# Low halves of weight blocks computed on GpSimd outside the recurrences; memory attention's softmax over two query blocks at a time

## The chip, the cores and the metric

The kernel runs on one NeuronCore of a Trainium2 chip. The metric is device time in microseconds (us) of one execution. Engines are named as in the profile: PE (matmul) with its weight loads PEld, DVE (vector), ACT (scalar), POOL (GpSimd) and SP, which here issues every DMA. SBUF is the on-chip memory of tiles, PSUM the banks into which PE accumulates.

## The reference, cut to what matters

Two layers. In each, one input projection feeds four branches, which are gated, projected, merged and normalised:

```python
for l in range(DEPTH):                       # DEPTH = 2, S = 512 tokens, D = 1024
    h = x @ w_in[l]                          # columns split among the branches
    y_rwkv = rwkv7(...)                      # delta-rule recurrence, 8 heads of 64
    y_mla  = causal_attention(...)           # low-rank latents, 8 heads
    h_c    = val * sigmoid(glu_gate)         # conformer branch
    y_conv = silu(layer_norm(causal_conv31(h_c))) * silu(gate)
    s      = q @ k_mem.T * 128 ** -0.5       # memory attention: 4 heads, 256 memory tokens
    y_mem  = softmax(s) @ v_mem * silu(gate)
    merged = sum(sigmoid(gate_n) * (y_n @ w_o[l, n]) for n in range(4))
    x      = layer_norm(ALPHA * x + merged @ w_out[l])
```

Everything is float32 in the reference.

## The kernel before, in words

**Split products.** PE multiplies in float16, so each float32 operand is carried as two float16 tiles, a high half h and a low half lo, and a product is three matmuls (`mm3`: h times lo, h times h, lo times h). Activations are split once; weights arrive from HBM as float32 blocks and are split on the fly. The blocks are named w0 to w237 in the order in which they are fetched, nearly all of 128x1024 elements or, for the latent projections, of 128x672. The first (w0) and the last three (flag `last`) are split in two pieces, the others whole: 236 low halves up to w234, and 6 for the last three. PE works about 24 matmuls of 512 columns on one full block.

**A weight block's way.** `weights` allocates a raw tile (three buffers), issues the DMA on SP's queue and starts a small task. When the block has landed and one of four h/lo buffer pairs is free, `split` writes h = float16(32 raw) on ACT, then lo = 32 raw - h on DVE in one scalar_tensor_tensor instruction. PE then uses the block, and the raw buffer goes to the block that is three further on.

**What sets the order.** All engines run their instructions in program order. That order comes from a planner in the kernel itself (`Plan`, `Engine`): every instruction is booked with an estimated cost, tasks are generators that run when the planner's clocks say that their inputs are there, and PE's stream of projections is filled in between. In `Engine.__call__` stands the table of costs by engine and operation.

**Fillers.** The convolution is 30 taps for each of four channel groups, DVE instructions `cacc <- hpad, prm, cacc` of 128x512. They are booked as "slack": one at a time when the planner thinks that DVE is free. Four `cacc` finished, `conv_norm` transposes and normalises them, and then the gates and merge products of the convolution's branch can be put on PE.

**The recurrences.** In each layer `begin_rwkv` opens the recurrence's pool and eight units of `rwkv_unit` follow, each with an inverse of 16x16 blocks by forward substitution on POOL (`ZT`, `tmpW`: 28 small instructions a unit). In the profile POOL's work of the two recurrences lies from 270 to some 510 us and from 1020 to some 1280 us. Apart from that POOL does only the reciprocal roots of the norms (`rstd_of`: `rsl` of the latents, `crs` of the convolution, `gr` of the recurrence, `lrs` of the layer's end).

**Memory attention.** `xhead` takes two query blocks of 128 at a time: PE writes both score blocks into one PSUM tile `xs` (128x2x256), and `weigh` makes the softmax of one block after the other: negative maximum `nm` (DVE), exponent with row sum `sm` (ACT), scaled reciprocal (two small DVE instructions), high half of the probabilities (ACT), low half (DVE). Then two DMA transposes bring them into `xT`, which PE reads for `xo`. `weigh` also serves the latent attention (`ms`, `mP`), where it gets one block.

Of the kernel before, what the change touches and what calls it, by code (L numbers as in the profile page):

```python
# [16 lines left out]
AF = mybir.ActivationFunctionType  # L17
ALU = mybir.AluOpType
# [18 lines left out]
WH = 8  # L37
WSCALE = 32.0
PROB = 16384.0
HEADS = 2  # L40
# [210 lines left out]
class Engine:  # L251
# [5 lines left out]
    def __getattr__(self, name):  # L257
        f = getattr(self.eng, name)

        def call(*a, **k):  # L260
            o = k.get("out", a[0] if a else None)
            i = k.get("in_", k.get("in0", a[1] if len(a) > 1 else o))
            n = 1
# [5 lines left out]
            if self.key == "ACT":  # L269
                c = (150 if psum else 115) + 0.83 * n + (150 if regs > 1 else 90 if regs or "accum_out" in k else 0)  # L270
            elif self.key == "POOL":
                c = 420 + 155 * n if k.get("op") == ALU.pow else 235 + 3.5 * n if n < 100 else 250 + 1.6 * n
            elif name == "scalar_tensor_tensor":
                c = 130 + 1.07 * n
            elif name in ("tensor_scalar", "tensor_copy"):
                c = (100 + 0.95 * n if psum else 68 + 0.53 * n) + (145 if regs else 0)
            elif name == "tensor_tensor_scan":
                c = 140 + 2.0 * n
            elif name == "bn_aggr":
                c = 66 + n  # L280
            else:
                c = 75 + 1.04 * n
# [65 lines left out]
def build(ctx: ExitStack, tc: tile.TileContext, A, out, log, slots, dbg=None):  # L348
# [178 lines left out]

    def split(dst_h, dst_l, src, scale=1.0):

        if scale == 1.0:  # L530
            S.copy(dst_h, src)
        else:
            S.activation(dst_h, src, AF.Copy, scale=scale)
        yield
        if scale == 1.0:
            V.tensor_tensor(out=dst_l, in0=src, in1=dst_h, op=ALU.subtract)
        else:
            V.scalar_tensor_tensor(out=dst_l, in0=src, scalar=scale, in1=dst_h, op0=ALU.mult, op1=ALU.subtract)

# [10 lines left out]

    whole = [1]

    def weights(name, src, parts, last=False):
# [8 lines left out]
        def run():  # L562
            e, n = 0, len(parts)
            step = 1 if whole[0] or last else n
            whole[0] = 0
            for a in range(0, n, step):
# [8 lines left out]
                h, lo = h[:, 0:c], lo[:, 0:c]  # L575
                yield from split(h, lo, raw[:, e:e + c], WSCALE)
                e += c
# [158 lines left out]
    def layer_items(l):  # L736
# [66 lines left out]
        def begin_rwkv(get):  # L803
# [64 lines left out]
        def rwkv_unit(j, hf, r, k, v):  # L868
# [444 lines left out]
        def weigh(h, lo, ps, tag):  # L1313

            nm, sm = st("nm" + tag, 1), st("sm" + tag, 1)
            V.tensor_reduce(out=nm, in_=ps, axis=AX.X, op=ALU.max, negate=True)
            yield
            S.activation(ps, ps, AF.Exp, bias=nm, accum_out=sm)
            yield
            V.tensor_scalar(out=sm, in0=sm, scalar1=1.0 / PROB, scalar2=None, op0=ALU.mult)  # L1320
            V.reciprocal(sm, sm)
            yield
            S.activation(h, ps, AF.Copy, scale=sm)
            yield
            V.scalar_tensor_tensor(out=lo, in0=ps, scalar=sm, in1=h, op0=ALU.mult, op1=ALU.subtract)

        ymem = [None] * 4

        def xhead(h, q):
# [3 lines left out]
            for tp in range(2):  # L1333
# [814 lines left out]
```

## Time and profile before

| | |
|---|---|
| median of 3 runs | 1455.22 us (1454.55 to 1455.3) |
| profiled execution, own time | 1457.4 us |
| its span, first to last instruction | 1455.6 us |
| PE busy | 1396.6 us (96%) |
| DVE busy | 1069.8 us (73%) |
| ACT busy | 650.3 us (45%) |
| POOL busy | 242.2 us (17%) |
| mean granted PE clock | 0.985 |

The own time is that of the whole execution, the span is counted from the first to the last instruction; 1.8 us lie around it. In the views a row of a group gives line, engine, operation, output<-inputs, shape and count, then busy time and mean duration of one. A tile's row gives shortest, median and longest duration. L285 is the planner's recording helper, so vector, scalar and GpSimd instructions are told apart by their tiles; L370 and L375 are matmuls and transposes.

### The profile page before, as it was taken

The numbers are of one execution on the slowest core, as the hardware profiler recorded it, in microseconds if no ns is written. First come the engines' busy times: TensorE is split into PE (matmuls) and PEld (weight loads), VectorE is DVE, ScalarE is ACT, GpSimd is POOL, SyncE is SP. The second block draws the span as 40 slices with busy tenths as digits, with TensorE's granted clock in tenths as the row PEclk, the third lists the DMA queues.
The fourth block names the chain that finished last, engine by engine and source line by source line (L and its number), as shares of the span: only waits on it lengthen the run. The fifth ranks groups of instructions, "written<-read, shape, count | busy, mean of one in ns | idle before, by whom it ended". The sixth has DMA issues, their size and how long they took to land. (4 is left out here: it accounts for less than half of the span.)

```text
span 1455.6 us, 29966 instructions
## 1 busy us (share of the span) xinstructions
PE 1396.6 (96%) x12134; PEld 754.1 (52%) x12134; DVE 1069.8 (73%) x2186; ACT 650.3 (45%) x1227; POOL 242.2 (17%) x557
## 2 busy tenths in 40 slices
PE   9999989999999789999999998999999998998997
PEld 6655544455555554444775544444455555554444
DVE  6688878888787876446654888888888868745756
ACT  5556564444443333344265556634444434432340
POOL 0000000355152600000010000000743433110001
PEclk9999999999999989999999999999999999999999
DMA  6445675231321024233443347662122221324331
GB/s 224 147 117 134 143 139 160 68 115 49 114 70 63 7 101 165 98 116 120 137 156 106 98 116 152 140 175 83 65 94 79 87 81 61 106 90 144 132 116 58
DMA packets 126539, 161.04 MB, mean 111 GB/s; under 512 B 83776, under 2 KB 85312, under 8 KB 126400
## 3 DMA queue, kind: packets, MB, share of 16 engines
q1 hardware_dynamic: 126400, 159.12, 36.6%
q8 instruction: 95, 1.56, 0.4%
q14 instruction: 44, 0.36, 0.1%
HBM read 133.39 MB, written 5.24 MB: 95 GB/s over the span
## 5 line engine op out<-in xcount | busy, mean ns | idle before, releaser
L285 DVE SCALAR_TENSOR_TENSOR cacc<-hpad,prm,cacc 128x512 f32<-128x512 f32 x240 | 179.9, 752 | 2.7
L285 ACT ACTIVATE tm<-ps_m,prm 128x512 f32<-128x512 f32 x64 | 44.0, 687 | 190.9 <-PE ps_m L370 180.2
L285 POOL TENSOR_SCALAR ZT<-W 32x256 f32<-32x256 f32 x16 | 12.2, 761 | 588.6 <-DMA W<-scr 362.5
L285 DVE SCALAR_TENSOR_TENSOR mt<-tm,po 128x512 f32<-128x512 f32 x48 | 32.9, 686 | 102.7 <-PE po L370 72.4
L285 POOL TENSOR_TENSOR ZT<-ZT,tmpW 32x14 f32<-32x14 f32 (+6 forms) x224 | 92.8, 414 | 17.6
L285 POOL TENSOR_TENSOR tmpW<-ZT,W 32x14 f32<-32x14 f32 (+6 forms) x224 | 92.3, 412 | 15.6
L370 PEld LDWEIGHTS <-mg 128*128 128x128 f16 x504 | 49.3, 98 | 34.0
L285 ACT ACTIVATE ms<-ms,nmm 128x128 f32<-128x128 f32 (+3 forms) x64 | 32.1, 501 | 18.4 <-DVE nmm L285 18.2
L285 ACT ACTIVATE mP<-ms,smm 128x128 f16<-128x128 f32 (+3 forms) x64 | 33.0, 527 | 13.5 <-issue 8.5
L370 PE MATMUL ms<-kT,qT 96*128 96x128 f16 (+3 forms) x192 | 36.3, 300 | 2.1 <-DMA kT<-xk 1.7
L285 ACT COPY Y<-gb 64x256 f32<-64x256 f32 x32 | 11.7, 367 | 57.6 <-DVE B L285 57.4
L285 POOL TENSOR_SCALAR gr<-gm 128x4 f32<-128x4 f32 x16 | 6.8, 423 | 179.0 <-DVE gm L285 179.0
L285 DVE TENSOR_TENSOR merged<-merged,mt 128x512 f32<-128x512 f32 x48 | 33.7, 703 | 1.7
L285 DVE SCALAR_TENSOR_TENSOR mP<-ms,smm,mP 128x128 f16<-128x128 f32 (+3 forms) x64 | 34.2, 544 | 0.0
L285 POOL TENSOR_SCALAR lrs<-lmv 128x1 f32<-128x1 f32 x4 | 2.2, 543 | 181.5 <-DVE lmv L285 177.3
L370 PEld LDWEIGHTS <-xh 128*128 128x128 f16 x256 | 25.0, 98 | 13.8 <-issue 2.5
L285 DVE TENSOR_REDUCE nmm<-ms 128x1 f32<-128x128 f32 (+3 forms) x64 | 30.4, 481 | 0.8 <-PE ms L370 0.2
L370 PEld LDWEIGHTS <-qT 96*128 96x128 f16 x192 | 17.1, 98 | 17.1 <-issue 3.5
L285 POOL TENSOR_TENSOR lrs<-lrs,mhalf 128x1 f32<-128x1 f32 x8 | 5.9, 742 | 107.0 <-DVE lrs L285 106.7
L285 DVE SCALAR_TENSOR_TENSOR z<-pz,z 128x256 f32<-128x256 f32 (+1 forms) x15 | 7.7, 512 | 20.9 <-PE pz L370 20.9
L285 ACT ACTIVATE mg<-merged 128x512 f16<-128x512 f32 x16 | 10.1, 630 | 28.1 <-DVE merged L285 28.1
L285 DVE SCALAR_TENSOR_TENSOR merged<-tm,po 128x512 f32<-128x512 f32 x16 | 11.0, 686 | 14.2 <-PE po L370 9.3
(1959 smaller groups left out, 4471.3 us busy)
## 6 DMA issues: line engine op xcount, KB each, us to landing
w<-in_w_ch_dram SPq DMA_DIRECT2D x146, 512.0 KB, 4.0
w<-in_w_o_dram SPq DMA_DIRECT2D x32, 512.0 KB, 3.9
w<-in_w_out_dram SPq DMA_DIRECT2D x16, 512.0 KB, 3.4
w<-in_w_lat_dram SPq DMA_DIRECT2D x16, 336.0 KB, 3.7
w<-in_w_mk_dram SPq DMA_DIRECT2D x8, 512.0 KB, 4.1
w<-in_w_mv_dram SPq DMA_DIRECT2D x8, 512.0 KB, 3.4
w<-in_w_qk_dram SPq DMA_DIRECT2D x8, 320.0 KB, 3.4
x<-in_xT_dram SPq DMA_DIRECT2D x8, 256.0 KB, 5.7
```

The costliest lines, as they stand in the source:

```text
L285: return self.plan.keep(f(*a, **k))
L370: plan.keep(nc.tensor.matmul(o, lhsT, rhs, start=start, stop=stop))
```

## The change

**1. Low halves on POOL.** `split` gets a function W. Where W says yes and the planner's clock of POOL is less than POOLED = 4000 ns ahead, lo is made by two POOL instructions instead of one on DVE: raw is multiplied by 32 in place, then lo = raw - h. `weights` passes `not busy and step > 1`: `busy` holds the layer from `begin_rwkv` to the end of its last unit, and step is 1 for the kernel's first block and its last three.

**2. Memory attention.** `weigh` takes the whole tile `xs` of two query blocks: one maximum for both, two exponents, one scaling and one reciprocal for both, two high halves, two low halves.

**3. Planner's costs.** Four of DVE's estimates are other numbers: scalar_tensor_tensor of 1000 elements and more, reciprocal, bn_aggr, and tensor_reduce from SBUF.

```diff
+POOLED = 4000.0
-                c = 130 + 1.07 * n
+                c = 130 + (1.07 if n < 1000 else 1.01) * n
+            elif name == "reciprocal":
+                c = 165
-                c = 66 + n
+                c = 170 + 4 * n
+            elif name == "tensor_reduce" and not psum:
+                c = 250 + 1.04 * n
...
-    def split(dst_h, dst_l, src, scale=1.0):
+    def split(dst_h, dst_l, src, scale=1.0, W=None):
...
-            V.scalar_tensor_tensor(out=dst_l, in0=src, scalar=scale, in1=dst_h, op0=ALU.mult, op1=ALU.subtract)
+            if W and W() and plan.clk["POOL"] < plan.now() + POOLED:
+                G.tensor_scalar(out=src, in0=src, scalar1=scale, scalar2=None, op0=ALU.mult)
+                G.tensor_tensor(out=dst_l, in0=src, in1=dst_h, op=ALU.subtract)
+            else:
+                V.scalar_tensor_tensor(out=dst_l, in0=src, scalar=scale, in1=dst_h, op0=ALU.mult, op1=ALU.subtract)
...
-                yield from split(h, lo, raw[:, e:e + c], WSCALE)
+                yield from split(h, lo, raw[:, e:e + c], WSCALE, lambda: not busy and step > 1)
...
+            busy.add(l)
...
+                busy.discard(l)
...
-            nm, sm = st("nm" + tag, 1), st("sm" + tag, 1)
+            parts = [(ps, h, lo)] if len(ps.shape) == 2 else [(ps[:, b, :], h[:, 256 * b:256 * b + 256], lo[:, 256 * b:256 * b + 256]) for b in range(2)]
+            nm, sm = st("nm" + tag, len(parts)), st("sm" + tag, len(parts))
             V.tensor_reduce(out=nm, in_=ps, axis=AX.X, op=ALU.max, negate=True)
             yield
-            S.activation(ps, ps, AF.Exp, bias=nm, accum_out=sm)
+            for b, (x, _, _) in enumerate(parts):
+                S.activation(x, x, AF.Exp, bias=nm[:, b:b + 1], accum_out=sm[:, b:b + 1])
...
-                for b in range(2):
-                    yield from weigh(P[:, 256 * b:256 * b + 256], P[:, 256 * b + 512:256 * b + 768], ps[:, b, :], f"x{h}{tp}{b}" + t_)
+                yield from weigh(P[:, 0:512], P[:, 512:], ps, f"x{h}{tp}" + t_)
```

In the changed program's order 125 of the low halves stand on POOL as pairs: w1 to w44, w101 to w166 and w220 to w234, without a gap, which is every block outside the two recurrences but the first and the last three. The other 111 of the 236, and the last 6, stay on DVE.

**How the order moves.** On POOL at the program's start, before (w blocks are raw weights, `rsl` is the latents' reciprocal root, `ZT` the first unit of the recurrence):

```order
L285 MEMSET dpad1_132 128x4
L285 ISA
L285 TENSOR_TENSOR rsl_0_626<-ssl_0_556,cst_81 128x8
L285 TENSOR_SCALAR rsl_0_626<-rsl_0_626 128x8
L285 TENSOR_TENSOR rsl_0_626<-rsl_0_626,mhalf_125 128x8
L285 TENSOR_SCALAR ZT_0_3058<-W_0_3057 32x256
```

The same place in the changed program:

```order
L290 MEMSET dpad1_132 128x4
L290 ISA
L290 TENSOR_SCALAR w1_150<-w1_150 128x672
L290 TENSOR_TENSOR w1l0_196<-w1_150,w1h0_195 128x672
L290 TENSOR_SCALAR w2_169<-w2_169 128x672
L290 TENSOR_TENSOR w2l0_249<-w2_169,w2h0_248 128x672
L290 TENSOR_SCALAR w3_220<-w3_220 128x672
L290 TENSOR_TENSOR w3l0_260<-w3_220,w3h0_259 128x672
```

POOL had nothing to do until the latents' norm; now ten pairs, w1 to w10, stand ahead of `rsl` and 34 behind it, up to the first `ZT`.

On DVE in the first layer, where the first attention pair is projected (`vm` values of the memory, `xq` and `xk` low halves of queries and keys, `cacc` taps), before:

```order
L285 SCALAR_TENSOR_TENSOR vm1_0_445<-pmv110_1094,vm1_0_445 128x256
L285 SCALAR_TENSOR_TENSOR w23l0_1171<-w23_1168,w23h0_1170 128x640
L285 SCALAR_TENSOR_TENSOR xq_0_1197<-pq0_0_1182,xq_0_1197 128x512
L285 SCALAR_TENSOR_TENSOR w24l0_1176<-w24_1173,w24h0_1175 128x1024
L285 SCALAR_TENSOR_TENSOR xk_0_1209<-pk0_0_1193,xk_0_1209 128x512
L285 SCALAR_TENSOR_TENSOR w25l0_1207<-w25_1204,w25h0_1206 128x1024
```

And in the changed program:

```order
L290 SCALAR_TENSOR_TENSOR vm1_0_439<-pmv110_1132,vm1_0_439 128x256
L290 SCALAR_TENSOR_TENSOR cacc0_0_781<-hpad0_127,prm0_236,cacc0_0_781 128x512 x2
L290 SCALAR_TENSOR_TENSOR xq_0_1233<-pq0_0_1215,xq_0_1233 128x512
L290 SCALAR_TENSOR_TENSOR xk_0_1245<-pk0_0_1229,xk_0_1245 128x512
L290 SCALAR_TENSOR_TENSOR cacc0_0_781<-hpad0_127,prm0_236,cacc0_0_781 128x512 x3
L290 SCALAR_TENSOR_TENSOR cacc1_0_1152<-hpad1_128,prm0_236,cacc1_0_1152 128x512 x3
```

The weight splits are gone and taps stand in their place: ahead of the first layer's recurrence (its first instruction on DVE, the copy into `V`) there are 91 taps instead of 52, ahead of the second's 90 of that layer's instead of 67. The first layer's fourth `cacc` is now finished in the third unit of the recurrence and not in the last but one.

On POOL at the end of the first layer (`lrs` is the reciprocal root of the layer norm of one token block), in the changed program:

```order
L290 TENSOR_SCALAR w124_8758<-w124_8758 128x1024
L290 TENSOR_TENSOR w124l0_8761<-w124_8758,w124h0_8760 128x1024
L290 TENSOR_SCALAR lrs0_0_8797<-lmv0_0_8796 128x1
L290 TENSOR_TENSOR lrs0_0_8797<-lrs0_0_8797,mhalf_125 128x1
L290 TENSOR_SCALAR w125_8775<-w125_8775 128x1024
L290 TENSOR_TENSOR w125l0_8780<-w125_8775,w125h0_8779 128x1024
L290 TENSOR_SCALAR lrs1_0_8831<-lmv1_0_8830 128x1
L290 TENSOR_TENSOR lrs1_0_8831<-lrs1_0_8831,mhalf_125 128x1
```

Before, the eight `lrs` instructions stood there by themselves; now the first two norms have a pair of a weight block ahead of them.

More of the change, by code (lines that the diff above doesn't have):

```diff
@@ L549, in build @@
     wlive = {"raw": 0, "hl": 0}
-    whole = [1]
+    whole, busy = [1], set()
     def weights(name, src, parts, last=False):
@@ L1322, in weigh @@
             yield
-            S.activation(h, ps, AF.Copy, scale=sm)
+            for b, (x, y, _) in enumerate(parts):
+                S.activation(y, x, AF.Copy, scale=sm[:, b:b + 1])
             yield
-            V.scalar_tensor_tensor(out=lo, in0=ps, scalar=sm, in1=h, op0=ALU.mult, op1=ALU.subtract)
+            for b, (x, y, z) in enumerate(parts):
+                V.scalar_tensor_tensor(out=z, in0=x, scalar=sm[:, b:b + 1], in1=y, op0=ALU.mult, op1=ALU.subtract)
         ymem = [None] * 4
```

## The prediction

> **What bounds the kernel now.** I read the page first: busy shares of the engines.
>
> ```profile
> span 1455.6 us, 29966 instructions
> PE 1396.6 (96%) x12134; PEld 754.1 (52%) x12134; DVE 1069.8 (73%) x2186; ACT 650.3 (45%) x1227; POOL 242.2 (17%) x557
> ```
>
> PE is idle for 1455.6 - 1396.6 = 59.0 us. The change leaves PE's matmuls as they are, so what it can win lies in these 59 us and in slow clock. The second view is what PE waited for, longest first:
>
> ```profile
> PE xo L370 <- DMA xTl<-xP: 6.8, 5, 2.4
> PE w L370 <- DVE cn L285: 2.5, 1, 2.5
> PE pmv L370 <- DVE w126l L285: 1.9, 1, 1.9
> PE tk L375 <- DVE cn L285: 1.3, 1, 1.3
> PE ct L375 <- DVE cn L285: 1.2, 1, 1.2
> PE ps_val L370 <- DVE w11l L285: 1.1, 1, 1.1
> PE pl L370 <- DVE w0l L285: 0.9, 1, 0.9
> PE pl L370 <- DVE w2l L285: 0.6, 1, 0.6
> PE ps_m L370 <- DVE w162l L285: 0.2, 1, 0.2
> ```
>
> Low halves of weights ended only 1.9 + 1.1 + 0.9 + 0.6 + 0.2 = 4.7 us of PE's waits. The work that moves is therefore not itself what PE waits for; a gain must come through DVE's other work. The third view is busy time by stage: the stretches ahead of the two recurrences (convolution and attentions) and the end of the first recurrence. Columns are stretch, length, then busy time of PE, PEld, DVE, ACT, POOL, and the granted clock.
>
> ```profile
> 55.00:265.00 210.00, 202.09 (x1335) 108.57 (x1334) 174.64 (x368) 119.90 (x255) 0.00 (x0) 0.99 0.56 136
> 480.00:535.00 55.00, 43.01 (x850) 28.93 (x847) 41.93 (x121) 17.61 (x37) 20.66 (x55) 0.84 0.18 58
> 800.00:1010.00 210.00, 198.88 (x1244) 99.88 (x1243) 180.73 (x377) 113.88 (x245) 0.00 (x0) 0.99 0.50 125
> ```
>
> Ahead of the recurrences DVE is busy 83 and 86% and idle 35.4 and 29.3 us; POOL does nothing. At 480 to 535 us PE stands idle for 12.0 us at a clock of 0.84: there the first recurrence's last units run with little else to put on PE.
>
> **DVE and POOL at the same time.** The one place where the trace shows both with much to do is the recurrence. First the durations by tile (shortest/median/longest in ns), then the rows around 400 us (start, duration, engine):
>
> ```profile
> L285 DVE TENSOR_TENSOR merged<-merged,mt x48: 691/692/1152, 399.5 to 1407.1; 128x512 f32<-128x512 f32 x48
> L285 POOL TENSOR_SCALAR ZT<-W x16: 605/712/1124, 270.2 to 1264.7; 32x256 f32<-32x256 f32 x16
> L285 POOL TENSOR_TENSOR tmpW<-ZT,W x224: 203/299/1417, 271.2 to 1281.8; 32x14 f32<-32x14 f32 x16, 32x36 f32<-32x36 f32 x16, 32x50 f32<-32x50 f32 x16, 32x56 f32<-32x56 f32 x16
> ```
>
> ```profile
> 399.48 0.61 POOL L285 TENSOR_SCALAR ZT<-W 32x256 f32<-32x256 f32 x1 [10.13 <-DMA W<-scr]
> 399.48 1.15 DVE L285 TENSOR_TENSOR merged<-merged,mt 128x512 f32<-128x512 f32 x1
> 400.91 1.23 DVE L285 SCALAR_TENSOR_TENSOR w70l<-w,w70h 128x1024 f16<-128x1024 f32 x1
> 401.13 1.11 POOL L285 TENSOR_TENSOR tmpW<-ZT,W 32x26 f32<-32x26 f32 x1
> ```
>
> A DVE instruction that reads two SBUF tiles and a POOL instruction do not run together. `merged` took 1.15 us instead of 0.69 while POOL's 0.61 us ran: it lost 0.46, POOL's length less 0.15. The other way round, `tmpW` on 26 columns took 1.11 us because w70's low half was running. Until now POOL's instructions were short, so DVE lost little. The change puts 250 long ones there, and the fillers that take the place of the weight splits on DVE, the taps `cacc <- hpad, prm, cacc`, read two SBUF tiles each.
>
> The Trainium skill, SBUF — State Buffer, section Who interferes with whom, says the same more strictly: the shared port pair is locked for the whole instruction and the other engine blocks fully. By that the loss would be the whole POOL instruction, 0.15 us more at each meeting, and the sum below about 12 us higher; the row with 0.46 of 0.61 decides for the smaller figure.
>
> **Price of a pair on POOL.** No row shows 128x1024 on POOL. The nearest, without DVE in the way:
>
> ```profile
> 349.71 0.22 POOL L285 TENSOR_TENSOR tmpW<-ZT,W 32x14 f32<-32x14 f32 x1
> 478.65 0.31 POOL L285 TENSOR_TENSOR tmpW<-ZT,W 32x56 f32<-32x56 f32 x1
> L285 POOL TENSOR_SCALAR crs<-cmv 128x1 f32<-128x1 f32 x8 | 1.5, 191 | 25.4 <-DVE cmv L285 25.3
> 398.08 1.06 ACT L285 ACTIVATE w70h<-w 128x1024 f16<-128x1024 f32 x1 [0.54 <-DMA w<-in_w_o_dram]
> ```
>
> The subtraction: (0.31 - 0.22)/42 = 2.1 ns a column, so 0.31 + 968 x 2.1 ns = 2.4 us; from below, 1.23 us, what DVE needs for the same tile. The multiplication: from 191 ns at one column to 605 at 256, 1.62 ns a column, so 1.85 us at most (strided there); from below, ACT's 1.06. I take 2.4, since it is the same operation on the same engine, and 1.4, about the middle, since ZT's source is strided. A pair is then 3.8 us, between 2.3 and 4.3, against 1.2 on DVE.
>
> By the Trainium skill, GPSIMD Engine Reference, section 3. Performance versus the Vector engine, a two-input add of 2048 elements takes 4497 ns; an estimate from that is 2.25 us for the subtraction, and with its near line-rate for one input about 1.05 for the multiplication. With these the sum below would be about +2 instead of +19; no run here shows either.
>
> **The change part by part.** Loss of DVE by a pair: between the convolution's first product and the recurrence the changed order has 321 DVE instructions, 114 of which read two SBUF tiles: a chance of 0.36 each. One lasts 174.64/368 = 0.47 us in the mean. Behind a POOL instruction of length P, DVE loses P - 0.15 if its next instruction is such a one, 0.47 less for each other instruction that comes first. For 2.4 us that is 0.36 x 2.25 + 0.23 x 1.78 + 0.15 x 1.31 + 0.09 x 0.84 + 0.06 x 0.37 = 1.5 us, for 1.4 us 0.7, together 2.2, and with DVE busy 83% of the time 1.8 us a block. What DVE is spared, and what the taps cost:
>
> ```profile
> 60.00:265.00 205.00, 0.00 (x0) 0.00 (x0) 40.89 (x36) 35.15 (x36) 0.99 0.56 135
> 800.00:1010.00 210.00, 0.00 (x0) 0.00 (x0) 38.28 (x33) 32.65 (x33) 0.99 0.50 125
> L285 DVE SCALAR_TENSOR_TENSOR cacc<-hpad,prm,cacc 128x512 f32<-128x512 f32 x240 | 179.9, 752 | 2.7
> L285 DVE TENSOR_REDUCE nmx<-xs 128x1 f32<-128x256 f32 x32 | 13.2, 416 | 0.7 <-PE xs L370 0.7
> L285 DVE RECIPROCAL smx<-smx 128x1 f32<-128x1 f32 x32 | 5.2, 164 | 1.1
> L285 DVE TENSOR_SCALAR smx<-smx 128x1 f32<-128x1 f32 x32 | 4.6, 144 | 0.0
> ```
>
> The first two rows are the weight instructions alone in the two stretches: 40.89/36 = 1.14 and 38.28/33 = 1.16 us of DVE a block.
>
> *First stretch*, blocks w14 to w44, 31 pairs: loss 31 x 1.8 = +56; splits gone -31 x 1.14 = -35; the joint softmax halves the small instructions, (5.2 + 4.6)/2 over two layers, and spares a maximum's fixed part (416 ns - 256 columns at 1.04, 0.15 us, eight times), about -4 a layer; 39 taps come in from the recurrence, 39 x 0.75 = +29. DVE's load grows by 46 us and 35.4 were idle. An engine that is behind doesn't wait any more, so I let three quarters of the idle time take it up, 26: DVE, and PE which needs DVE to empty PSUM, come out +20 us late. Bounds: 46 - 35 = +11 and +46.
>
> *Second stretch*, w140 to w166, 27 pairs: +49 - 31 - 4 + 23 taps x 0.75 = +17 makes +31, against 29.3 idle, three quarters 22: +9, between +2 and +31.
>
> *Start*: w1's and w2's low halves are on PE's path.
>
> ```profile
> 8.05 0.76 ACT L285 ACTIVATE w1h<-w 128x672 f16<-128x672 f32 x1 [0.20 <-DMA w<-in_w_lat_dram]
> 8.85 0.86 DVE L285 SCALAR_TENSOR_TENSOR w1l<-w,w1h 128x672 f16<-128x672 f32 x1
> 9.86 0.31 PE L370 MATMUL pl<-w1l,xh 128*128 128x336 f16 x1
> 13.11 0.86 DVE L285 SCALAR_TENSOR_TENSOR w2l<-w,w2h 128x672 f16<-128x672 f32 x1 [0.35 <-ACT w2h L285]
> ```
>
> PE takes w1l 0.15 us after it is ready. A pair on 672 columns is some 2.6 us instead of 0.86, so +2 once (0.3 to 4); w2 then comes in PE's shifted time.
>
> *First layer's end*: the first two of four `lrs` now stand behind a pair on POOL, with DVE's `lnb` and the layer's last transposes behind them, and low halves come 3.8 - 1.2 = 2.6 us later. Two rows show the margin between a low half's start and PE's first use:
>
> ```profile
> L285 DVE SCALAR_TENSOR_TENSOR w110l<-w,w110h x1: 1219/1219/1219, 677.9 to 677.9; 128x1024 f16<-128x1024 f32 x1
> L370 PE MATMUL po<-yrg,w110l x8: 379/379/379, 679.4 to 683.9; 128*128 128x512 f16 x8
> ```
>
> w110 has 0.3 us, most others some us; +2 here (0 to 8). In the same row eight matmuls of a third each span 4.5 us, so PE works 5.1 us on a block; POOL's 3.8 keeps up, and nothing is added in steady projection. The raw buffer is released 2.6 us later, and with it the DMA of the third block on, with DMA transposes behind it on SP's queue; blocks are fetched two to three ahead, some 10 us, so 0, up to 3 where they aren't.
>
> *What is won*: the convolution is done in the recurrence's third unit, so PE's waits on `cn` (2.5 + 1.3 + 1.2 = 5.0) go, and its gates and merges can fill part of the other 7 us idle and lift the clock at 480 to 535: -11 (-5 to -16). The softmax chain loses one round of hand-overs per pair: of the 6.8 us on `xT` -3 (0 to -5). The planner's new costs are no work; their effect is the order already counted.
>
> Sum: +20 + 9 + 2 + 2 - 11 - 3 = +19 us. The profiled execution took 1457.4 us, which makes 1476; by the median of 1455.2 it is 1474.
>
> **Rivals.** *DVE gains after all* (faster). Should POOL's instructions on plain rows run near the lower bound, 1.06 and 1.23 us, the loss is 0.36 x 0.91 + 0.23 x 0.44 and 0.36 x 1.08 + 0.23 x 0.61 + 0.15 x 0.14, or 0.8 us a block with DVE's share; then the stretches' loads grow by 46 - 31 = +15 and 31 - 27 = +4 us, idle time hides both, and -14 with 1 at the start remain: 1442. It decides at a loss of 1.8 - 19/58 = 1.5 us a block, 58 blocks in both stretches. For it: no POOL row is on plain 128 partitions. Against it: the slope of 2.1 ns.
>
> *No change*: the loss is 1.5 us, what DVE is late is what the convolution wins: 1455.
>
> *POOL is the bound* (slower by more): each instruction of a pair also waits for a tap in progress, as `tmpW` did up to 1417 ns. With 6.0 us a pair against PE's 5.1, the 40 blocks w101 to w125 and w220 to w234 add 36, and a loss of 2.5 us a block adds 0.7 x 58 = 41: about 1550. For it, the longest rows; against it, DVE reads two SBUF tiles less often there.
>
> That the change doesn't take place is out: the order shows the 125 pairs.
>
> **How the numbers follow.** Forecast 0.49, faster rival 0.28, no change 0.12, POOL as bound 0.11. The forecast's own range, from the bounds of the two stretches, with the other terms as they are, is 1458 to 1520. The range over all cases, 1440 to 1520, reaches down to the faster rival and leaves out most of the last rival and the lower part of the faster one. A measurement here tells 0.2%, 3 us, from no change: faster 0.28, same 0.12, slower 0.49 + 0.11 = 0.60.
>
> **What would show it.** Right: `cacc` and `merged` with means or long tails well above 752 and 692 ns outside the recurrences; a pair near 3.8 us; PE waits on DVE and on POOL's low halves at 60 to 265 and 800 to 1010 us; fewer idle us where the first recurrence ends. Wrong: `cacc` unchanged at 0.75 us, DVE's busy time down by over 100 us, or the two stretches no longer than before.

## The result, and the profile after

The changed kernel takes 1525.33 us in the median of four runs (1519.08 to 1529.82) against 1455.26 us before: a ratio of 1.0481, 95% interval 1.0451 to 1.0510, slower. The forecast was 1474 with a range of 1440 to 1520: the sign is right, the size is not (+19 forecast, +70 measured). The profiled execution took 1526.58 us, its span is 1524.8 us. First the head of the page of the changed kernel, and from its second part POOL's busy tenths in 40 slices of 38 us:

```profile
span 1524.8 us, 30283 instructions
PE 1412.6 (93%) x12134; PEld 755.4 (50%) x12134; DVE 1056.8 (69%) x2013; ACT 652.0 (43%) x1227; POOL 832.3 (55%) x807
POOL 7997565464323230098989774457463241500992
```

PE is idle for 1524.8 - 1412.6 = 112.2 us, 53 more than before, and its same matmuls take 16.0 us longer at a mean granted clock of 0.977 instead of 0.985: 69 us in all. DVE is busy 13 us less only, though 125 splits of 1.14 us, 143 us, left it. POOL is busy nine tenths or more in the second and third slice, and eight tenths or more in slices 18 to 22. Now the groups and POOL's two new instructions:

```profile
L290 DVE SCALAR_TENSOR_TENSOR cacc<-hpad,prm,cacc 128x512 f32<-128x512 f32 x240 | 240.0, 1003 | 3.4
L290 DVE TENSOR_TENSOR merged<-merged,mt 128x512 f32<-128x512 f32 x48 | 39.3, 818 | 1.7
L290 POOL TENSOR_SCALAR w<-w x125: 1808/2771/3215, 8.4 to 1487.3; 128x1024 f32<-128x1024 f32 x100, 128x672 f32<-128x672 f32 x15, 128x640 f32<-128x640 f32 x8, 128x768 f32<-128x768 f32 x2
L290 POOL TENSOR_TENSOR w14l<-w,w14h x1: 2125/2125/2125, 73.7 to 73.7; 128x1024 f16<-128x1024 f32 x1
```

The same 240 taps take 60 us longer in all (752 ns became 1003 in the mean). The subtraction takes 2.1 us, close to what was forecast; the multiplication takes 2.8 us, twice the forecast. A pair is 4.9 us. What this does to DVE is seen where a chain of small steps runs, in the timeline (start, duration, engine; in brackets the idle time before and who ended it):

```profile
105.35 2.38 POOL L290 TENSOR_TENSOR w20l<-w,w20h 128x1024 f16<-128x1024 f32 x1
105.68 2.34 DVE L290 TENSOR_TENSOR qp<-rq 128x256 f32<-128x256 f32 x1
107.71 2.94 POOL L290 TENSOR_SCALAR w<-w 128x1024 f32<-128x1024 f32 x1
107.94 2.72 DVE L290 TENSOR_TENSOR v<-vf,v 128x512 f16<-128x512 f32 x3
108.07 0.44 PE L380 MATMUL qr<-cst,qp 128*128 128x128 f32 x2 [3.75 <-DVE qp L290]
```

`qp` came 0.33 us after POOL's subtraction had begun and ended 0.29 us after it: 2.34 us for an instruction that takes 0.41 when POOL is idle. It lost 1.93 us of the 2.05 that POOL still ran, which is the prediction's "length less 0.15" almost exactly. PE had waited 3.75 us for it. From the head of PE's waits:

```profile
PE qr L380 <- DVE qp L290: 7.1, 2, 3.8
PE ps_val L375 <- POOL w11l L290: 4.3, 1, 4.3
PE pmv L375 <- POOL w126l L290: 4.3, 1, 4.3
PE pk L375 <- DVE vm L290: 3.8, 1, 3.8
PE xo L375 <- DMA xTl<-xP: 3.6, 3, 2.4
PE pz L375 <- POOL w118l L290: 3.5, 1, 3.5
PE ps_xq L375 <- POOL w36l L290: 3.4, 1, 3.4
PE pz L375 <- POOL w123l L290: 2.5, 1, 2.5
```

Summed over the whole view, low halves that POOL makes end 61.0 us of PE's waits, and DVE 31.4. A wait names only who came last, and a late high half or a late tap lies behind many of them, so the sums don't divide the loss.

**Where the time went.** PE's work is the same, so the start of the first matmul on a block is a clock by which two kernels can be compared place by place. From before to after, the time from the first use of one block to that of the next named one changed by +12.0 us for w0 to w13, +32.8 for w14 to w44 (ahead of the first recurrence), +1.8 for w45 to w79, -22.1 for w80 to w100 (the first recurrence's end), +2.8 for w101 to w114, +19.9 for w115 to w125 (the first layer's end), +4.8 for w126 to w139, +30.4 for w140 to w166, -18.1 for w167 to w219 (second recurrence) and +4.9 from w220 on. Together that is +69.2.

### The profile page after: what moved, and what is told of

Read it like the earlier page. It is cut to its first block, busy times and chain, and to the rows that moved or that the text cites. A ratio compares the mean times of both kernels' runs of the same rounds, so it can differ in the third digit from the quotient of the medians.

```text
span 1524.8 us, 30283 instructions
## 1 busy us (share of the span) xinstructions
PE 1412.6 (93%) x12134; PEld 755.4 (50%) x12134; DVE 1056.8 (69%) x2013; ACT 652.0 (43%) x1227; POOL 832.3 (55%) x807
## 5 line engine op out<-in xcount | busy, mean ns | idle before, releaser
L290 POOL TENSOR_SCALAR w<-w 128x1024 f32<-128x1024 f32 (+3 forms) x125 | 344.0, 2752 | 173.2 <-ACT w153h L290 16.9
L290 DVE SCALAR_TENSOR_TENSOR cacc<-hpad,prm,cacc 128x512 f32<-128x512 f32 x240 | 240.0, 1003 | 3.4
L290 POOL TENSOR_TENSOR tmpW<-ZT,W 32x14 f32<-32x14 f32 (+6 forms) x224 | 96.1, 429 | 15.3
L290 POOL TENSOR_TENSOR ZT<-ZT,tmpW 32x14 f32<-32x14 f32 (+6 forms) x224 | 83.8, 374 | 17.5
L290 ACT ACTIVATE ms<-ms,nmm 128x128 f32<-128x128 f32 (+3 forms) x64 | 31.9, 499 | 28.8 <-DVE nmm L290 28.2
L290 DVE TENSOR_TENSOR merged<-merged,mt 128x512 f32<-128x512 f32 x48 | 39.3, 818 | 1.7
L290 ACT ACTIVATE mP<-ms,smm 128x128 f16<-128x128 f32 (+3 forms) x64 | 32.4, 527 | 11.1 <-issue 6.0
L375 PEld LDWEIGHTS <-qT 96*128 96x128 f16 x192 | 16.9, 99 | 18.1 <-issue 4.9
L375 PEld LDWEIGHTS <-mem 128*128 128x128 f16 x192 | 19.4, 101 | 11.5 <-issue 8.4
L290 DVE SCALAR_TENSOR_TENSOR S<-w,De,H 128x64 f32<-128x64 f32 x48 | 13.3, 276 | 15.7 <-PE w L375 15.5
```

Of the source, the lines that this page charges most:

```text
L290: return self.plan.keep(f(*a, **k))
L375: plan.keep(nc.tensor.matmul(o, lhsT, rhs, start=start, stop=stop))
```

## The experiments

Theories at the outset: **hold-up**, called lock in the first expectations (POOL's long instructions hold up DVE's, and PE waits for DVE; the prediction's own), **pace**, called late there (POOL needs 4.9 us a block, low halves and raw buffers come late; the rival "POOL is the bound"), **order** (the planner's new costs and the softmax).

### What is lost to POOL, in one order

Kernel without the pairs. The planner books them all the same, which leaves the order on PE, DVE and ACT as it is in the changed kernel.

```diff
-                G.tensor_scalar(out=src, in0=src, scalar1=scale, scalar2=None, op0=ALU.mult)
-                G.tensor_tensor(out=dst_l, in0=src, in1=dst_h, op=ALU.subtract)
+                plan.op("POOL", 250 + 1.6 * src.shape[1], _names(src), [])
+                plan.op("POOL", 250 + 1.6 * src.shape[1], _names(dst_l), _names(src, dst_h))
+                skip.add(dst_l.tensor.name)
+                plan.done[dst_h.tensor.name] = plan.done[dst_l.tensor.name]
...
-                    ws[i].extend((h[:, f:f + parts[i]], lo[:, f:f + parts[i]]))
+                    z = h if lo.tensor.name in skip else lo
+                    ws[i].extend((h[:, f:f + parts[i]], z[:, f:f + parts[i]]))
```

> The changed kernel without the 125 pairs on POOL: those low halves are not made at all, and PE multiplies by the high half in their place; the planner still books the pairs, so that the order on PE, DVE and ACT is the changed kernel's. Three theories for the +70 us. Lock: POOL's long instructions hold up DVE's instructions on two SBUF tiles, and PE waits for DVE. Late: a pair takes 4.9 us where PE needs 5.1 us a block, low halves come 4 us later than before and PE waits for them. Order: it is the new order (planner's costs, joint softmax), whatever runs on POOL. Lock and late both expect 1425 to 1445 us (before less the 59 us that PE was idle at most, with some idle time left); order expects at least 1490.

1407.95 us, ratio 0.9671 (0.9654 to 0.9689). PE multiplies by other values here, but its own pace is the same: from w101 to w109 it uses a block in 5.2 us in this kernel, in the changed one and in the one before. From its page:

```profile
span 1405.8 us, 29662 instructions
PE 1379.7 (98%) x12134; PEld 747.1 (53%) x12134; DVE 937.3 (67%) x2013; ACT 650.0 (46%) x1227; POOL 233.8 (17%) x557
L290 DVE SCALAR_TENSOR_TENSOR cacc<-hpad,prm,cacc 128x512 f32<-128x512 f32 x240 | 179.6, 751 | 3.4
```

As both theories on POOL expected, but lower: with splits that cost nothing, softmax and costs, the change would gain 47 us, and the changed order as such is good. The pairs on POOL cost 1525.3 - 1408.0 = 117 us. DVE has the same 2013 instructions in both; in the changed kernel they are busy 1056.8 - 937.3 = 119.5 us longer.

**Pairs made but not read.** The two POOL lines stay, the rest of the edit is the one above.

> The changed kernel with its 125 pairs on POOL, in the same order on every engine, but PE multiplies by the high half in place of these low halves, so that it never waits for POOL; the low halves are made and not read. Lock expects 1500 to 1525 us, nearly all of the loss, with cacc at a mean of 1.0 us. Late expects 1430 to 1460, most of the loss gone, though cacc is as long as in the changed kernel. Order expects 1500 to 1525 and the same as the kernel without pairs.

1509.24 us, ratio 1.0359 (1.0343 to 1.0376). PE now waits on DVE and ACT:

```profile
PE pqe L375 <- DVE vm L290: 6.1, 1, 6.1
PE ps_mk L375 <- ACT z L290: 6.1, 1, 6.1
PE qr L380 <- DVE qp L290: 5.9, 2, 4.9
PE pz L375 <- ACT w123h L290: 3.3, 1, 3.3
```

101 of the 117 us remain: without PE's direct wait for low halves only 16 come back. This is what hold-up expects. But waits on high halves such as `w123h` say that raw buffers still come late, and ACT's `z` had itself waited for DVE's `lnb`, which waited for POOL's root `lrs`, so the run doesn't tell hold-up from pace as cleanly as it was meant to.

**Pairs on tiles of POOL's own.** Raw buffers are released by ACT alone; each subtraction reads the high half, to come at its time.

```diff
...
+                plan.keep(nc.gpsimd.tensor_tensor(out=scl[:, 0:src.shape[1]], in0=scr[:, 0:src.shape[1]], in1=dst_h, op=ALU.subtract))
+                plan.keep(nc.gpsimd.tensor_scalar(out=scr[:, 0:src.shape[1]], in0=scr[:, 0:src.shape[1]], scalar1=1.0, scalar2=None, op0=ALU.mult))
...
```

> As the kernel without the 125 pairs (their low halves left out, PE multiplying by the high half, same order on PE, DVE and ACT), but POOL runs 125 pairs of the same forms on tiles of its own: each subtraction reads the block's high half, so that it comes at its time, the multiplication follows; raw buffers no longer wait for POOL. Nothing but the pairs' presence is left, besides a high half's buffer that is held until the subtraction is done. Without pairs this kernel takes 1408 us, with pairs on the real tiles, unread, 1509. If DVE's hold-up is the cause: 1490 to 1510. If it is raw buffers released late by POOL, and so DMAs and high halves: 1410 to 1440.

1520.37 us, ratio 1.0427 (1.0401 to 1.0453), against pace and over what hold-up expected. Late raw buffers are out. But a high half's buffer was still held until POOL had subtracted, and DVE waited for POOL's small roots:

```profile
DVE lnb L290 <- POOL lrs L290: 21.7, 4, 19.4
```

**Pairs that no buffer waits for.** ACT copies one column after each high half into a tile of its own; POOL reads it, then subtracts and multiplies on spare tiles.

```diff
+                f = cp.pool.tile([128, 1], F32, tag=f"fl{len(flags)}", name=f"fl{len(flags)}")
+                plan.keep(nc.scalar.copy(f, src[:, 0:1]))
...
+                plan.keep(nc.gpsimd.tensor_scalar(out=tick, in0=f, scalar1=1.0, scalar2=None, op0=ALU.mult))
+                plan.keep(nc.gpsimd.tensor_tensor(out=scl[:, 0:n], in0=scr[:, 0:n], in1=scl[:, 0:n], op=ALU.subtract))
+                plan.keep(nc.gpsimd.tensor_scalar(out=scr[:, 0:n], in0=scr[:, 0:n], scalar1=1.0, scalar2=None, op0=ALU.mult))
...
```

> The kernel without the 125 pairs (their low halves left out, PE multiplying by the high half), with 125 pairs of the same forms on tiles of POOL's own that no buffer waits for: a one-column copy by ACT after each high half, in a tile of its own, tells POOL when to start, and POOL may fall behind without holding up a raw buffer or a high half. If DVE's hold-up makes nearly all of the 101 to 112 us that unread pairs cost: 1490 to 1515. If POOL's pace of 4.9 us a block made half or more of it: 1430 to 1460, with the time between first uses of w14 and w25 back at 45 to 52 us from 65.

1523.01 us, ratio 1.0443 (1.0413 to 1.0472), above the range for hold-up. The waits of DVE, and the timeline where the first layer ends, show a third way:

```profile
DVE lnb L290 <- POOL lrs L290: 23.4, 4, 21.0
DVE latq L290 <- POOL rsl L290: 21.7, 2, 11.8
```

```profile
779.73 0.19 POOL L290 TENSOR_SCALAR lrs<-lmv 128x1 f32<-128x1 f32 x1
780.01 0.57 POOL L290 TENSOR_TENSOR lrs<-lrs,mhalf 128x1 f32<-128x1 f32 x1
780.61 0.16 DVE L290 SCALAR_TENSOR_TENSOR lnb<-lmv,lrs 128x1 f32<-128x1 f32 x1 [21.02 <-POOL lrs L290]
```

A free-running POOL falls behind, and the small roots of the norms stand behind the pairs in its queue: 0.8 us of work came 21 us late. That is a **queue**, neither pace for the low halves nor hold-up. The changed kernel hardly has it: there DVE waits for `lrs` 0.4 us in all, for `rsl` 9.5 against 6.1 in the kernel without pairs. So two more kernels, the one without pairs and this one, both with `rsl` and `lrs` left out (a constant from one small DVE instruction in their place):

```diff
+        if here:
...
+            plan.keep(nc.vector.tensor_scalar(out=dst, in0=src, scalar1=0.0, scalar2=0.01, op0=ALU.mult, op1=ALU.add))
+            return
```

> The kernel without the 125 pairs (low halves left out), and with the reciprocal roots rsl and lrs left out as well: one small DVE instruction writes a constant in their place, so that nothing outside the recurrences and the convolution's norm waits for POOL. It serves as the base of the next: 1398 to 1408 us, since it loses POOL's 1.65 us root twice and four short ones.

> The same with the 125 free pairs on POOL. No buffer, and now no latent and no layer norm waits for them: what it takes longer than the kernel above is DVE's hold-up alone (with ACT's 125 one-column copies). If the small roots behind late pairs made 35 to 40 us of the free pairs' 115: 75 to 85 us longer, 1475 to 1490, and w115 to w126 back at 40 to 45 us from 62. If the hold-up made it all: 105 to 115 longer, 1505 to 1520.

The base takes 1409.98 us (ratio 0.9674, 0.9659 to 0.9690), just above what was expected: these roots cost nothing without pairs. With free pairs it is 1494.56 us (1.0254, 1.0233 to 1.0274). **DVE's hold-up alone costs 85 us**, the 75 to 85 that its first branch expected; the other 30 us of the free pairs were the queue. ACT's 125 one-column copies, 22.7 us of ACT's time, are in the 85, but it is DVE that PE waits for: what DVE ends of PE's waits goes from 6.7 to 60.2 us, what ACT ends from 4.0 to 9.3. `cacc` here, and the two longest of PE's waits:

```profile
L290 DVE SCALAR_TENSOR_TENSOR cacc<-hpad,prm,cacc 128x512 f32<-128x512 f32 x240 | 258.5, 1080 | 3.4
PE qr L380 <- DVE qp L290: 11.5, 3, 5.6
PE pqe L375 <- DVE vm L290: 6.1, 1, 6.1
```

**The same POOL time without a hold-up.** Memsets of about the same length in place of each pair. PE waits for the low half and the raw buffer is held as in the changed kernel; the low halves are zero.

```diff
...
+                plan.keep(nc.gpsimd.tensor_copy(tick[:, 0:1], dst_h[:, 0:1]))
+                for _ in range(4):
+                    plan.keep(nc.gpsimd.memset(scr[:, 0:n], 1.0))
+                plan.keep(nc.gpsimd.tensor_copy(tick[:, 1:2], src[:, 0:1]))
+                plan.keep(nc.gpsimd.memset(dst_l, 0.0))
...
```

> The changed kernel with each pair replaced by POOL memsets of about the same length, 4.9 us (a one-column copy that waits for the high half, four memsets of a spare tile, a one-column copy of the raw block, which is released with it, and a memset of the low half to zero, for which PE waits as before; the low halves' values are left out). A memset reads no SBUF. If it doesn't hold DVE up, cacc stays at 0.75 us and what remains over 1408 is POOL's pace and lateness alone: 1415 to 1440 if DVE's hold-up is the cause, 1455 to 1500 if the pace is half of it or more. If cacc gets as long as with pairs, a memset holds DVE up as well: 1510 to 1530, which settles only that.

1494.84 us, ratio 1.0272 (1.0250 to 1.0293). Its groups and waits:

```profile
L290 DVE SCALAR_TENSOR_TENSOR cacc<-hpad,prm,cacc 128x512 f32<-128x512 f32 x240 | 179.3, 750 | 3.4
L549 POOL MEMSET scr<- 128x1024 f32 x400 | 381.2, 953 | 17.2
```

```profile
PE ps_val L375 <- POOL w11l L551: 4.8, 1, 4.8
PE pmv L375 <- POOL w126l L551: 3.9, 1, 3.9
PE pz L375 <- POOL w123l L551: 3.6, 1, 3.6
PE ps_xq L375 <- POOL w36l L551: 3.5, 1, 3.5
```

The taps are as short as without pairs: a memset doesn't hold DVE up, so the prediction's sentence that such a DVE instruction and a POOL instruction do not run together is too wide. By the Trainium skill, SBUF — State Buffer, section Who interferes with whom, a DVE instruction with two SBUF inputs is in conflict with a GpSimd instruction that reads SBUF, not with one that only writes it; the 750 ns agree. **POOL's pace alone costs 1494.8 - 1408.0 = 87 us.** POOL's low halves end 65.0 us of PE's waits here, DVE 7.1. The memsets of a full block with their copies take 5.1 us in the median, a little more than a pair, so 87 may be slightly high. The theory that hold-up is the cause and pace a trifle falls with this run.

**Both, place by place.** Time between first uses of blocks, in the kernel without pairs, and how much longer it is in the others (for hold-up alone against its own base). The first row counts from the start of the span, and in it lie some 5.4 us before PE's first matmul.

| blocks | without pairs | pace alone | hold-up alone | changed kernel |
|---|---|---|---|---|
| w0 to w13 | 58.4 | +16.2 | +1.7 | +15.7 |
| w14 to w24 | 44.8 | +13.5 | +23.8 | +20.6 |
| w25 to w44 | 138.0 | +10.5 | +17.7 | +17.0 |
| w45 to w114 | 434.8 | +2.2 | +0.7 | +2.8 |
| w115 to w125 | 39.8 | +21.7 | +2.0 | +23.0 |
| w126 to w139 | 64.1 | +2.7 | +4.3 | +2.9 |
| w140 to w166 | 178.1 | +16.7 | +37.3 | +32.3 |
| w167 to the end | 447.8 | +2.0 | 0.0 | +4.7 |
| span | 1405.8 | +85.5 | +87.5 | +119.0 |

Four of the rows behind it, from the kernel without pairs and then from the changed one (behind the colon: shortest, median and longest duration in ns, then the first and last start in us):

```profile
L375 PE MATMUL ps_glu<-xl,w14h x8: 379/379/379, 58.4 to 62.9; 128*128 128x512 f16 x8
L375 PE MATMUL ps_xq<-xl,w25h x8: 376/378/379, 103.2 to 109.6; 128*128 128x512 f16 x8
L375 PE MATMUL ps_mk<-mem,w116h x24: 272/273/273, 678.7 to 681.2; 128*128 128x256 f16 x24
L375 PE MATMUL pz<-w118h,mg x48: 272/273/273, 682.6 to 691.7; 128*128 128x256 f16 x48
```

```profile
L375 PE MATMUL ps_glu<-xl,w14h x8: 379/379/379, 74.1 to 80.0; 128*128 128x512 f16 x8
L375 PE MATMUL ps_xq<-xl,w25h x8: 376/378/379, 139.5 to 145.9; 128*128 128x512 f16 x8
L375 PE MATMUL ps_mk<-mem,w116h x16: 272/273/273, 734.8 to 739.1; 128*128 128x256 f16 x16
L375 PE MATMUL pz<-w118l,mg x16: 269/273/421, 746.7 to 757.3; 128*128 128x256 f16 x16
```

The two losses don't add up. At most places the changed kernel loses about the larger of the two. Pace decides at w0 to w13 and w115 to w125. Of the 16.2 us in the first row 4.1 come before w2, by the first low halves, and 11.2 from w8 to w13, where PE uses a block in 25.1/6 = 4.2 us, less than a pair's 4.9; the blocks before have 672 columns, and a pair there takes 1.9 + 1.5 = 3.4 us, as long as PE takes. At w115 to w125 PE uses a block in 39.8/11 = 3.6 us in the mean, but w116 and w117 together in 3.9, and with pairs in 11.9. Hold-up decides from w14 to w44 and w140 to w166, where the taps and the attentions' small steps run on DVE. From w14 to w24 PE uses a block in 44.8/11 = 4.1 us and both are at work.

### Shorter or fewer POOL instructions

ACT multiplies, POOL subtracts only:

```diff
-                G.tensor_scalar(out=src, in0=src, scalar1=scale, scalar2=None, op0=ALU.mult)
+                S.activation(src, src, AF.Copy, scale=scale)
```

> The changed kernel, but ACT multiplies the raw block by 32 in place, and POOL does the subtraction alone, 2.1 us instead of 4.9. If DVE's hold-up is the cause, its price goes with the length of POOL's instructions: 2.1/4.9 of the 101 us that pairs cost when nothing reads them, 43 us on 1408, and little waiting for low halves: 1445 to 1465. If low halves and raw buffers that come late are the cause: 1410 to 1435, since h and lo are done 4.3 us after h's start and POOL is far from PE's 5.1 us a block.

1465.42 us, ratio 1.0071 (1.0044 to 1.0098), just over what hold-up expects and far from pace's 1410 to 1435. The planner, which books less for POOL here, gives it 128 blocks instead of 125. Of the free pairs, the subtractions alone:

> As the free pairs, with the subtraction alone, 2.1 us a block. DVE's hold-up by length gives 2.1/4.9 of what the free pairs cost, at a hold-up worth 100 us 1450, at one worth 50 us 1430. If this is well under the 1465 of the kernel in which ACT multiplies and POOL subtracts, the rest there was ACT's extra 1.06 us a block or the wait for low halves.

1451.32 us, ratio 0.9966 (0.9953 to 0.9979): 43 us over 1408 for 2.1 us a block, where the 85 us of the whole pair by length would be 2.1/4.9 x 85 = 36. The taps are 980 ns in the mean, seven tenths of the lengthening that the free pairs bring, so the price doesn't go by length alone. The other 14 us of the kernel in which ACT multiplies are ACT's extra instruction or the wait for low halves, which end 9.8 us of PE's waits there; that wasn't separated.

Pieces of 256 columns in the changed kernel. The planner books more for them and so leaves 13 blocks on DVE: 112 are cut into pieces, and the order is a little different.

```diff
+                for c in range(0, src.shape[1], 256):
+                    e = min(c + 256, src.shape[1])
+                    G.tensor_scalar(out=src[:, c:e], in0=src[:, c:e], scalar1=scale, scalar2=None, op0=ALU.mult)
+                    G.tensor_tensor(out=dst_l[:, c:e], in0=src[:, c:e], in1=dst_h[:, c:e], op=ALU.subtract)
```

> The changed kernel, with each pair cut into pieces of 256 columns, eight POOL instructions of some 0.6 to 0.8 us instead of two of 2.8 and 2.1. If DVE is held up for one whole POOL instruction at a time and comes in between two of them, cacc's mean falls from 1.00 us towards 0.85 and the time to 1465 to 1500. If POOL being late is the cause: 1530 to 1560, since pairs become longer by the pieces' fixed parts and by DVE's instructions that come between.

1552.08 us, ratio 1.0651 (1.0622 to 1.0680). Of each expectation a half came, hold-up's shorter taps and pace's longer time, in the groups and the waits:

```profile
L290 DVE SCALAR_TENSOR_TENSOR cacc<-hpad,prm,cacc 128x512 f32<-128x512 f32 x240 | 204.9, 856 | 3.4
L290 POOL TENSOR_SCALAR w<-w 128x256 f32<-128x256 f32 x404 | 397.4, 984 | 75.1 <-ACT w153h L290 11.3 <-ACT w155h L290 10.4 <-ACT w1h L290 7.5
```

```profile
PE pz L375 <- POOL w118l L290: 5.0, 4, 1.7
PE pmv L375 <- POOL w16l L290: 4.7, 4, 1.2
```

DVE does come in between pieces, and taps fall to 0.86 us. But the 404 multiplications of 256 columns take 397 us where 125 whole ones took 344, so pace gets worse, and PE waits for low halves. What is given to one bound is taken by the other.

Every second block only:

```diff
-                yield from split(h, lo, raw[:, e:e + c], WSCALE, lambda: not busy and step > 1)
+                yield from split(h, lo, raw[:, e:e + c], WSCALE, lambda: not busy and step > 1 and int(name[1:]) % 2)
```

> The changed kernel with a pair for every second block alone (odd numbers); the others' low halves stay on DVE. DVE's hold-up should go with the number of long POOL instructions, and a block left on DVE costs what it costs without pairs: half-way between 1440.6 without pairs and 1525 with all, 1475 to 1495. If POOL falling behind were what counts (4.9 us a block against PE's 5.1), half the pairs would leave POOL idle half of the time and nothing late: 1440 to 1455.

1470.16 us, ratio 1.0084 (1.0063 to 1.0105): between the two expectations. 65 pairs of 125 cost 30 us over the 1440.6 with none, less than half of the 85 that all cost. A pair on every second block leaves POOL twice the time, so pace may be what went; it wasn't taken apart further.

ACT's multiplication and POOL's subtraction for 34 blocks away from the worst places, then for 35 spread over both stretches (what is added to the condition `not busy and step > 1`):

```diff
+ and (25 <= int(name[1:]) < 45 or 126 <= int(name[1:]) < 140)
```

```diff
+ and int(name[1:]) % 2 and (14 <= int(name[1:]) < 45 or 126 <= int(name[1:]) < 167)
```

> The kernel without pairs (1440.6 us), but for w25 to w44 and w126 to w139 ACT multiplies and POOL does the subtraction alone. These are blocks between the places where the changed kernel lost most (w1 to w24, w115 to w125, w155 to w166). If DVE's hold-up costs something only where DVE's work is what PE waits for: 1425 to 1440, as the convolution is done earlier and the recurrences' ends (w80 to w100, w185 to w219) shorten. If a hold-up costs wherever it falls: 34 subtractions at (1465 - 1408)/125 = 0.46 us each, less 0.26 us spared on DVE, so 1445 to 1455.

> As the one before, but every second block of w14 to w44 and w126 to w166, about as many subtractions spread over the whole of both stretches. If place decides: slower than the one before by 5 to 15 us, 1440 to 1450. If number decides: within 4 us of it.

1445.91 us (0.9935, 0.9923 to 0.9947) and 1448.16 us (0.9950, 0.9935 to 0.9966). By what was expected of each, number decides more than place, though the orders differ too: 83 and 75 taps stand ahead of the two recurrences in the first, 70 and 76 in the second. Neither reaches the 1440.63 us of the kernel with no pairs at all.

### The parts of the change that are not on POOL

Pairs off (W is `None`); pairs alone on the kernel before; the joint softmax alone; the four costs alone.

```diff
-                yield from split(h, lo, raw[:, e:e + c], WSCALE, lambda: not busy and step > 1)
+                yield from split(h, lo, raw[:, e:e + c], WSCALE, None)
```

> The changed kernel with every low half on DVE again: joint softmax and the planner's new costs alone. Lock and late both expect 1445 to 1458 us, about the kernel before or a little under it, since the joint softmax removes small instructions. Order expects 1490 to 1530.

> The kernel before with the pairs on POOL alone: old softmax, old costs. Lock and late expect 1515 to 1535 us, as the changed kernel. Order expects 1455 to 1480.

> The kernel before with the joint softmax of memory attention alone: old costs, low halves on DVE. Joint softmax and new costs together gave 1440.6 against 1457.5. If the gain is the shorter softmax (fewer hand-overs, 4 us less of DVE a layer): 1440 to 1446. If it is the order that the new costs make: 1452 to 1458.

> The kernel before with the planner's four new costs alone: old softmax, low halves on DVE. Softmax and costs together took 1440.6 us against 1457.5, softmax alone 1452.1 against 1456.4. If the two add up: 1443 to 1447. If the costs only help once the softmax is shorter: 1452 to 1458.

| | us | ratio, 95% interval |
|---|---|---|
| no pairs: softmax and costs | 1440.63 | 0.9894 (0.9878 to 0.9911) |
| pairs alone | 1532.18 | 1.0513 (1.0490 to 1.0537) |
| softmax alone | 1452.06 | 0.9971 (0.9958 to 0.9984) |
| costs alone | 1475.21 | 1.0124 (1.0104 to 1.0144) |

Order as the cause is out: pairs alone lose what the changed kernel loses, and without pairs the changed kernel is the fastest here that leaves nothing out, 17 us under the kernel before and below what was expected of it. But the two other parts don't add up: the softmax alone gains 4 us, the costs alone lose 17, outside both expectations, and together they gain 17. In the kernel with the costs alone PE waits for the convolution at both recurrences' ends, the longest at the second's, in the waits:

```profile
PE cb L379 <- DVE cn L289: 5.9, 2, 4.2
PE ct L379 <- DVE cn L289: 5.0, 2, 2.7
```

With costs and softmax `cb` waits 0.4 us for `cn`. The taps ahead of the two recurrences are 52 and 67 in the kernel before, 52 and 51 with the costs alone, 70 and 71 with the softmax alone, 62 and 71 with both: the costs alone do put fewer taps ahead of the second recurrence. But 12.1 of their 17 us are lost at w140 to w166, ahead of it, so these waits are only a part of it, and the cause of the rest stays open.

## Why the prediction was wrong

**What held.** DVE's taps lengthen outside the recurrences (752 to 1003 ns, `merged` 703 to 818), PE waits on DVE and on low halves where the stretches were named, and the convolution's waits at the first recurrence's end go. The estimate of a loss of 1.8 us a block came near, with luck: with the hold-up alone, the same DVE instructions are 53.6 us longer for the 31 blocks w14 to w44 and 48.1 us for the 27 blocks w140 to w166, 1.7 and 1.8 us a block, but the 1.8 was worked out for instructions of 2.4 and 1.4 us, and with the measured 2.1 and 2.8 the same formula gives 2.6. In the changed kernel, where POOL's pace spaces the pairs out, it is 42.9 and 31.9 us, 1.4 and 1.2.

**Step that failed first: "POOL's 3.8 keeps up, and nothing is added in steady projection".** The pair is 4.9 us: 2.1 for the subtraction (2.4 taken) and 2.8 for the multiplication (1.4 taken, 1.85 as the upper bound). The bound came from `ZT`, a 32x256 instruction of 605 ns; on 128 partitions 256 columns take 848 ns in the median in the kernel with pieces, so a row of another shape was no bound. By the Trainium skill, GPSIMD Engine Reference, section 4.1 Engine selection, a one-input operation on GPSIMD is roughly at line rate; 2.77 us for 1024 columns, longer than the two-input subtraction, says otherwise for this form. And PE's 5.1 us a block, read at w110, is not its pace everywhere: 4.2, 4.1 and 3.6 us at w8 to w13, w14 to w24 and w115 to w125. Where PE does take 5.2, from w101 to w109, even the pair of 4.9 keeps up and nothing is lost; where it takes two blocks in 3.9, a pair of 3.8 would have been late as well. Pace alone costs 87 us. The rival that named it gave +36 for it at blocks w101 to w125 and w220 to w234; right in kind, but of these places only w115 to w125 shows it.

**Second step: "three quarters of the idle time take it up".** DVE alone in w14 to w44 and in w140 to w166, from the kernel before and then with the hold-up alone (stretch, its length, DVE's busy time, granted clock, DMA share and GB/s):

```profile
62.10:249.67 187.57, 155.17 (x337) 0.99 0.60 143
809.87:989.89 180.02, 157.63 (x338) 0.99 0.57 139
```

```profile
59.93:284.43 224.50, 206.51 (x329) 0.93 0.50 119
830.00:1044.95 214.95, 198.60 (x323) 0.91 0.48 117
```

DVE's load grows by 51.3 and 41.0 us, where 46 and 31 were taken. Its idle time goes from 32.4 to 18.0 and from 22.4 to 16.4, so 14.4 and 6.0 us were taken up, less than half, where 26 and 22 had been counted. The stretches get 36.9 and 34.9 us longer by hold-up alone, where +20 and +9 were forecast; in the changed kernel, with pace, they are +32.8 and +30.4. Against its own base, PE comes 41.5 and 37.3 us later where DVE's instructions are 53.6 and 48.1 longer: three quarters reach PE. A reading of this, shown at the one place of the timeline, is that DVE's idle time lies between the steps of a chain (`qp`, then PE's `qr`, then DVE again), where a held step shifts the whole chain.

**Third: "Start" +2 and "First layer's end" +2.** The rows that were looked at came out: w2's first use is 2.9 us later, and w110, with its margin of 0.3 us, costs 2.4. What stood at nothing lies beside them: +9.1 for w2 to w13 and +19.9 for w115 to w125. How fast PE goes through the blocks there hadn't been looked at; both are pace, as the table shows. The roots behind pairs, which the term for the layer's end began with, cost nothing: DVE waits 0.4 us for `lrs`.

**What is won** was forecast at -11 and -3. It is -22.1 at w80 to w100 and -18.1 over the second recurrence, which had not been counted. But softmax and costs without any pair already give -15.8 and -7.4 there, with 62 and 71 taps ahead of the recurrences instead of 91 and 90, so the taps that the pairs make room for are at most the rest of it. The softmax alone brings 4 us, near the 3 taken for its hand-overs, but with the new costs 17; "the planner's new costs are no work; their effect is the order already counted" is true of the order and says nothing of its worth.

So the sum failed by a missing bound, 87 us where 0 stood, that lies in part over the 85 us of the bound that was seen: together 117 us, less the 47 that splits off DVE, softmax and costs gain: +70.

## What to carry to other kernels

Before work goes to another engine, price it there on a row of its own shape and compare its pace with the consumer's fastest stretch, not with its mean or a steady one. On GpSimd, work that reads SBUF is charged twice: in its own time, and in that of VectorE's instructions with two SBUF inputs; of what VectorE was held up, some three quarters reached TensorE here. Two bounds that cost 87 and 85 us alone cost 117 together, so removing one of them shows little, and a test has to take each away alone.

## What the runs showed of the hardware

- POOL's float32 multiplication in place takes 2.77 us on 128x1024 and 1.89 on 128x672, from which 2.5 ns a column and 0.2 us fixed are worked out; the two-input subtraction into float16 takes 2.1 and 1.5 us. The one with two inputs is the shorter.
- A POOL memset of 128x1024 float32 takes 0.95 us and leaves DVE's instructions with two SBUF inputs at 750 ns, where multiplications and subtractions make them 1003 to 1080 in the mean.
- PE's time in the same 12134 matmuls isn't fixed: 1379.7 us in the kernel without pairs (26.1 us idle, mean granted clock 0.996), 1412.6 us in the changed one (112.2 us idle, 0.977). The clock doesn't go by idle time alone: it is 0.990 with 58.1 us idle in the kernel with free subtractions, 0.986 with 45.6 in the one with softmax and costs only.
